# A third pair of FFN blocks as seven products, and both FFN projections in one sequence

## The chip, the cores and the metric

The kernel runs on one core of one Trainium2 chip. The metric is the device time of one execution in microseconds: 942.69 us is the median of three runs of the kernel before (941.98 to 943.01). Times inside an execution come from a profile of one run, counted from its first instruction (its span).

Names of the engines: PE is TensorE's matmul side and PEld its loading of the stationary operand, DVE is VectorE, ACT is ScalarE, POOL is GpSimd, SP is the engine whose queue issues the DMAs. L90 is line 90 of the kernel before.

## The reference

Two layers of a hybrid encoder over 256 tokens of width 1024, all in float32. A layer computes a combined projection, gated linear attention (GLA) and grouped-query attention, merges them, projects once more, and then does a feed-forward part (FFN) and an input embedding. What matters here is the FFN:

```python
def hybrid_layer(h, p_i, ...):
    ...
    gate, up = jnp.split(rms_norm(h, g_ffn_pre) @ w_ffn_in, 2, axis=-1)
    h = h + rms_norm((jax.nn.silu(gate) * up) @ w_ffn_out, g_ffn_post)

    e = p_i @ w_ple_proj
    h = h + rms_norm(jax.nn.sigmoid(h @ w_ple_gate) * e, g_ple_post)
    return h
```

The hidden width is 2816, so w_ffn_in is 1024 x 5632 (gate columns, then up columns) and w_ffn_out is 2816 x 1024.

## The kernel before, in words

**Precision.** Every float32 operand of a large matmul is split into a high and a low part (`split`, L104: a cast on ScalarE, L106, and a subtraction on VectorE, L102). A product is then three matmuls (`mm3`, L92): high by high, high by low, low by high. The tokens lie in two halves (hf 0 and 1) of 128, and an activation is the stationary operand: a matmul is 128x128 by 128x512.

**Weights.** `plan` (from L167) lists all weight units in the order of their use; a unit is 128 x 2048 numbers, 1 MB. `Stream` loads a unit by SP's queue into one of two raw buffers, splits it in two pieces of 1024 columns into a pair of buffers wh and wl (four of each), and hands it out with `take`; `done` frees the buffers and starts the split and the load of later units. Up to four units are held.

**FFN, first projection.** The hidden width is 11 blocks of 256 (`NBLK`). A plain block (`block`, L1219) takes 256 gate and 256 up columns as two units (one for each half of the contraction) and makes 48 matmuls of 512 columns; its results go through silu and a product (VectorE, L99), four 128x128 transposes on TensorE, and a split into `hid`, the transposed hidden state.

**Pairs.** Two blocks (b and b+1) can be done as one pair by Strassen's scheme in Winograd's form (`seven`, L559; `Stream.step`, L278): a 2x2 block product with seven products of 12 matmuls in place of eight. The seven weight operands are made from four loaded quarters by sums of 128 x 2048 on VectorE (L282 to L293), two of which lie in a wh and a wl buffer that is lent for them, one in a buffer of the pool `big`. The seven activation operands are quarters and four sums made once a layer (`sums`, L534). The products are combined by VectorE steps of 512 columns (L102, L566) and ScalarE copies (L583), and `gated` (L1251) turns each half into hidden state.

**The order.** Blocks 0 and 1 come first. Then `FFN_IN` (L35) is an order written out by hand: "u" is one unit of a plain block, the digits 1 to 7 are the products of a pair. `PLAIN` names the plain blocks (4, 5, 8, 9, 10), `PAIRS` the first blocks of the pairs (2 and 6). After it, rope_tables(l+1) and up_weights(l+1) make the next layer's small tables (layer 0 only), p is loaded and transposed (`turn_p_in`), and the second projection runs (`out_step`, L1294): 11 units, each with 12 matmuls for each half; the last four units are done by half, so that the post-norm of half 0 runs beside the matmuls of half 1.

**What else sets the order.** `tick` counts steps of TensorE's program; a `Task` does its next piece after the number of ticks that it yields (WAIT_PAIR is 9 ticks from a pair's gating to its transposes). Engine orders follow the program's order, except that work marked by `high_priority` goes earlier and work that is ready may be placed ahead of work that is not. Pools: `mid` has 10 buffers of 128 x 1024, `big` 9 of 128 x 2048, and PSUM 8 banks, shared by accumulators (`acc`) and transposes (`aux`).

Of the kernel before, what the change touches and what calls it, by code (L numbers as in the profile page):

```python
# [17 lines left out]
P = 128  # L18
T = 256
# [12 lines left out]
HIDDEN = 2816  # L32
NBLK = HIDDEN // 256

FFN_IN = "uu12u34u5u67uu12u34u5u67"  # L35
WAIT_PAIR = 9
PLAIN, PAIRS = (4, 5, 8, 9, 10), (2, 6)
UNIT = 2112
RQ = ((0, 288), (288, 672), (672, 1056))
C_GQ, C_GK, C_GV, C_GG, C_RA = 0, 512, 1024, 2048, 3072  # L40
# [4 lines left out]
def trunk_kernel(ctx: ExitStack, tc: tile.TileContext, a: dict, out: bass.AP):  # L45
# [107 lines left out]
    def unit_rows(w, n, c0=0, c1=D, parts=1):  # L153

        if parts == 2:
            return lambda t: [
                (t[:, k * (c1 - c0) : (k + 1) * (c1 - c0)], w[(2 * n + k) * P : (2 * n + k + 1) * P, c0:c1])
                for k in range(2)
            ]
        return lambda t: [  # L160
            (
                t[:, : 2 * (c1 - c0)].rearrange("p (k c) -> p k c", k=2),
                w[n * 256 : (n + 1) * 256, c0:c1].rearrange("(k p) c -> p k c", p=P),
            )
        ]

    plan = []  # L167
    for l in range(DEPTH):
        w = a["w_in"][l]
        plan += [unit_rows(w, n, C_RA, C_RA + 1056, 2 if l + n == 0 else 1) for n in range(4)]  # L170
        for c0 in (C_AK, C_GQ, C_GK, C_GV, C_GV + 512, C_GG, C_GG + 512, C_GA, C_GA + 512, C_GB, C_GB + 512):
            plan += [unit(w, kh, c0) for kh in range(2)]
        for j in range(2):
            for wo in (a["w_o_gla"][l], a["w_o_attn"][l]):
                plan += [unit(wo, kh, j * 512) for kh in range(2)]
        plan += [unit(a["w_out"][l], kh, j * 512) for kh in range(2) for j in range(2)]
        w = a["w_ffn_in"][l]
        blocks = [[unit_gate_up(w, kh, b) for kh in range(2)] for b in range(NBLK)]
        plan += blocks[0] + blocks[1]
        plains = [u for b in PLAIN for u in blocks[b]]  # L180
        pairs = [[unit(w, kh, c + b * 256) for kh in range(2) for c in (0, HIDDEN)] for b in PAIRS]
        for x in FFN_IN:
            if x == "1":
                pair = pairs.pop(0)
            plan.append(plains.pop(0) if x == "u" else (pair, int(x)))
        plan += [unit_rows(a["w_ffn_out"][l], n) for n in range(NBLK)]
        plan += [unit_rows(a["w_ple_proj"][l], 0)]
        plan += [unit(a["w_ple_gate"][l], kh, j * 512) for kh in range(2) for j in range(2)]

# [259 lines left out]
    def halves(t):  # L449
        return [t[:, j * 512 : (j + 1) * 512] for j in range(2)]  # L450
# [108 lines left out]
    def seven(sp, forms, gated):  # L559

        made, task = forms
        quad = lambda hf, j: lambda k: sp.tok(4 * j + k, hf)
        form = lambda i: lambda k: [p[:, k, :] for p in made[i]]

        def add(out, x, y):
            nc.vector.tensor_tensor(out=out, in0=x, in1=y, op=ALU.add)  # L566

        (p1, v), (p3, p7), (c12, c22) = (halves(mid()) for _ in range(3))
        c11 = acc()
        times(c11, quad(0, 0))  # L570
        nc.scalar.copy(p1, c11)
        yield
        task.need()
        o = acc()
        times(o, form(0))
        nc.scalar.copy(p3, o)
        yield
        p5 = acc()
        times(p5, form(1))
        yield  # L580
        o = acc()
        times(o, form(2))
        nc.scalar.copy(p7, o)  # L583
        yield
        o = acc()
        times(o, form(3))
        vsub(v, o, p1)
        add(v, p5, v)
        add(c12, v, p3)
        add(c22, v, p7)  # L590
        yield
        times(c11, quad(0, 1), False)
        gated(0, c11, c12)
        yield
        times(p5, quad(1, 1), False)
        vsub(v, p5, c22)
        gated(1, v, c22)
        yield
# [164 lines left out]
    for l in range(DEPTH):  # L763
# [399 lines left out]
        for j in range(2):  # L1163
            for br, src in enumerate((gT, aT)):
                for hf, o in enumerate(project(src)):
                    sl = [s[:, hf, j * 512 : (j + 1) * 512] for s in sgate]
                    vmul(sl[br], o, sl[br])
                    if br == 1:
# [5 lines left out]

                        mixT.makers[hf].append(Task(turn(), part[0], j))


        part[0] = f"{l}wout"
        gpost = gain(a["g_mix_post"][l], mid(), D)
# [70 lines left out]
        def pair(b):  # L1250
            def gated(hf, gate, up):  # L1251
                sg = t512()
                nc.scalar.activation(sg, gate, AF.Silu)
                vmul(sg, up, sg)
                turned(sg, 2 * b, 4, hf, WAIT_PAIR)

            return seven(u2, forms, gated)

        steps, pairs, seven_ = chain.from_iterable(block(b) for b in PLAIN), list(PAIRS), None
        for x in FFN_IN:  # L1260
            if x == "1":
                seven_ = pair(pairs.pop(0))
            next(steps if x == "u" else seven_)
        ws.lend = False

        if l + 1 < DEPTH:
            ropes = rope_tables(l + 1)
            wup_next = up_weights(l + 1)


        part[0] = f"{l}emb"
        pin = t512().rearrange("p (s c) -> p s c", c=256)
        nc.sync.dma_start(pin, a["p"][l, 0].rearrange("(s p) c -> p s c", p=P))
        pT = [t.rearrange("p (k t) -> p k t", t=T) for t in halves(mid(F32R))]

        def turn_p_in():
            yield 8
            ps = aux()
            for k in range(2):
                for hf in range(2):  # L1280
                    nc.tensor.transpose(
                        ps[:, k * T + hf * P : k * T + (hf + 1) * P], pin[:, hf, k * P : (k + 1) * P], ident
                    )
            split(pT[0], pT[1], ps.rearrange("p (k t) -> p k t", t=T))

        embedded = Task(turn_p_in(), part[0])


        part[0] = f"{l}ffnout"
        gpost = gain(a["g_ffn_post"][l], mid(), D)  # L1290
        gple = gain(a["g_ple_post"][l], mid(), D)
        o = [[acc(), acc()] for _ in range(2)]

        def out_step(n, hf, w):  # L1294
            wh, wl = (t[:, :2048].rearrange("p (k c) -> p k c", c=512) for t in w)
            for kk in range(2):
                k = 2 * n + kk
                hid.need(hf, k)
                for j in range(2):
                    mm3(  # L1300
                        o[hf][j], hid.tok(k, hf), (wh[:, 2 * kk + j, :], wl[:, 2 * kk + j, :]),
                        k == 0, k == 2 * NBLK - 1,
                    )
                tick()

        for n in range(NBLK - 4):
            w = ws.take()
            for hf in range(2):
                out_step(n, hf, w)
            ws.done()  # L1310
        us = [ws.take() for _ in range(4)]
        hT = Split()
        for hf in range(2):
            for n in range(4):
                out_step(NBLK - 4 + n, hf, us[n])
                if hf == 1:
                    ws.done()
            post_norm_add(o[hf], gpost, hf)

            turn_in(hT, h[:, hf, :], hf, WAIT_H)  # L1320
# [93 lines left out]
```

## Time and profile before

| What | us |
|---|---|
| median of three runs | 942.69 |
| the profiled execution, whole | 942.66 |
| its span, first to last instruction | 940.9 |
| chain of waits: TensorE's share | 85% |
| chain of waits: VectorE, DMA, ScalarE, POOL | 6%, 3%, 2%, 2% |
| one ScalarE cast of half a unit (128 x 1024) | 1.05 |
| one VectorE subtraction of half a unit | 1.22 |
| one VectorE sum of two quarters (128 x 2048) | 2.28 |
| landing of a 1 MB load of w_ffn_out | 4.8 to 6.4 |
| DMA, mean over the span | 180 GB/s |

In layer 0 the second pair's products run from 342.37 to 379.2 us, the second projection from 379.8 to 441.8 us. The chain of waits is the work that ended last, followed back step by step; the durations in the table are means of one instruction, and neighbours on an engine overlap by some 0.08 us.

### The profile page before, as it was taken

What the parts mean: (1) busy time and instruction counts of PE and PEld (TensorE: products, weight loads), DVE (VectorE), ACT (ScalarE), POOL (GpSimd) and SP (SyncE); (2) the same over time, 40 slices, a digit from 0 to 9 for tenths busy, and PEclk for the clock granted to TensorE, in tenths of its full rate; (3) what the DMA queues carried; (4) which work ended last, traced back from release to release, by engine and by line L of the source; (5) the groups of instructions that cost most, each with busy time, mean ns of one, the idle gap of its engine ahead of it and who ended that gap; (6) DMA issues with size and microseconds to landing.
All of it is one profiled execution on the core that took longest, in us unless ns stands there. A gap on an engine that the chain in (4) does not pass through costs nothing.

```text
span 940.9 us, 12357 instructions
## 1 busy us (share of the span) xinstructions
PE 927.7 (99%) x4721; PEld 788.9 (84%) x4721; DVE 695.6 (74%) x906; ACT 547.0 (58%) x916; POOL 90.2 (10%) x152
## 2 busy tenths in 40 slices
PE   8999999999999999999999999999999999999996
PEld 7998888888878888888889988888888788888886
DVE  5798977456679999755779799674666798996374
ACT  5569676434466666444656686754436656664263
POOL 3500211000000000301032001200002000000010
PEclk9999999999999999999999999999999999999999
DMA  7463444655385554764545525365552937276531
GB/s 256 140 240 120 162 173 170 216 181 191 102 279 178 185 182 155 264 245 157 181 138 179 194 76 179 121 237 184 206 190 92 311 125 261 75 265 227 179 135 45
DMA packets 92313, 169.26 MB, mean 180 GB/s; under 512 B 3479, under 2 KB 34711, under 8 KB 92254
## 3 DMA queue, kind: packets, MB, share of 16 engines
q1 hardware_dynamic: 92254, 168.47, 52.5%
q8 instruction: 37, 0.61, 0.3%
q14 instruction: 22, 0.18, 0.1%
HBM read 167.41 MB, written 1.05 MB: 179 GB/s over the span
## 4 chain that ended last, share of the span: by engine, by line
PE 85%; DVE 6%; DMA 3%; ACT 2%; POOL 2%; issue 2%; SPq 0%; POOLq 0%; DVEq 0%; ACTq 0%
PE acc_1ffnout L90 6%; PE acc_0ffnout L90 6%; PE acc_1ffnin L90 6%; PE acc_0ffnin L90 6%; PE acc_0gate L90 5%; PE acc_1gate L90 5%; PE acc_1merge L90 5%; PE acc_0merge L90 5%; PE acc_0ffnin L527 4%; PE acc_1ffnin L527 3%; PE acc_1gqk L90 2%; PE acc_0gqk L90 2%; PE acc_1ple L90 2%; PE acc_1gg L90 2%; PE acc_0gg L90 2%; PE acc_1v L90 2%
## 5 line engine op out<-in xcount | busy, mean ns | idle before, releaser
L90 PE MATMUL acc_1ffnin<-wh_1ffnin,big_1wout 128*128 128x512 f32 x160 | 51.8, 394 | 0.0
L90 PE MATMUL acc_0ffnin<-wh_0ffnin,big_0wout 128*128 128x512 f32 x160 | 51.8, 394 | 0.0
L106 ACT CAST wh_1ffnin<-raw_1ffnin 128x1024 fp32r<-128x1024 f32 x28 | 27.9, 1049 | 16.2 <-PE acc_1ffnin L90 8.8
L102 DVE TENSOR_TENSOR wl_1ffnin<-raw_1ffnin,wh_1ffnin 128x1024 fp32r<-128x1024 f32 x28 | 32.9, 1218 | 5.1 <-ACT wh_1ffnin L106 5.1
L106 ACT CAST wh_0ffnin<-raw_0ffnin 128x1024 fp32r<-128x1024 f32 x28 | 27.9, 1048 | 14.8 <-PE acc_0ffnin L90 9.3
L102 DVE TENSOR_TENSOR wl_0ffnin<-raw_0ffnin,wh_0ffnin 128x1024 fp32r<-128x1024 f32 x28 | 33.2, 1226 | 3.2 <-ACT wh_0ffnin L106 3.1
L90 PEld LDWEIGHTS acc_0ffnin<-wh_0ffnin,big_0wout 128*128 128x128 f32 x160 | 30.0, 188 | 6.1
L90 PEld LDWEIGHTS acc_1ffnin<-wh_1ffnin,big_1wout 128*128 128x128 f32 x160 | 30.0, 188 | 6.1
L90 PE MATMUL acc_0ffnout<-wh_0ffnout,big_0ffnin 128*128 128x512 f32 x112 | 34.9, 390 | 0.0
L90 PE MATMUL acc_1ffnout<-wh_1ffnout,big_1ffnin 128*128 128x512 f32 x112 | 34.9, 390 | 0.0
L102 DVE TENSOR_TENSOR wl_1ffnout<-raw_1ffnout,wh_1ffnout 128x1024 fp32r<-128x1024 f32 x18 | 21.3, 1221 | 16.5 <-ACT wh_1ffnout L106 16.5
L90 PE MATMUL acc_0ffnin<-wl_0ffnin,big_0wout 128*128 128x512 f32 x80 | 31.2, 390 | 0.0
L90 PE MATMUL acc_1ffnin<-wl_1ffnin,big_1wout 128*128 128x512 f32 x80 | 31.2, 390 | 0.0
L106 ACT CAST wh_1ffnout<-raw_1ffnout 128x1024 fp32r<-128x1024 f32 x18 | 18.1, 1051 | 20.8 <-PE acc_1ffnout L90 15.5
L102 DVE TENSOR_TENSOR wl_0ffnout<-raw_0ffnout,wh_0ffnout 128x1024 fp32r<-128x1024 f32 x18 | 21.3, 1220 | 11.4 <-ACT wh_0ffnout L106 11.3
L102 DVE TENSOR_TENSOR wl_1gate<-raw_1gate,wh_1gate 128x1024 fp32r<-128x1024 f32 x14 | 16.5, 1222 | 17.8 <-ACT wh_1gate L106 17.8
L102 DVE TENSOR_TENSOR wl_0gate<-raw_0gate,wh_0gate 128x1024 fp32r<-128x1024 f32 x14 | 16.5, 1221 | 17.8 <-ACT wh_0gate L106 17.8
L106 ACT CAST wh_0ffnout<-raw_0ffnout 128x1024 fp32r<-128x1024 f32 x18 | 18.1, 1053 | 15.0 <-PE acc_0ffnout L90 7.7
L90 PE MATMUL acc_0rq<-wh_start,big_start 128*128 128x384 f32 (+1 forms) x96 | 24.5, 339 | 1.0 <-ACT big_start L116 0.9
L90 PE MATMUL acc_1gate<-wh_1gate,big_0ple 128*128 128x512 f32 x80 | 24.8, 389 | 0.0
L90 PE MATMUL acc_0gate<-wh_0gate,big_start 128*128 128x512 f32 x80 | 24.8, 389 | 0.0
L90 PEld LDWEIGHTS acc_0ffnout<-wh_0ffnout,big_0ffnin 128*128 128x128 f32 x112 | 21.0, 188 | 4.4
(653 smaller groups left out, 3026.0 us busy)
## 6 DMA issues: line engine op xcount, KB each, us to landing
raw_0ffnin<-in_w_ffn_in_dram SPq DMA_DIRECT2D x16, 512.0 KB, 5.9
raw_1ffnin<-in_w_ffn_in_dram SPq DMA_DIRECT2D x16, 512.0 KB, 6.3
raw_0ffnin<-in_w_ffn_out_dram SPq DMA_DIRECT2D x6, 1024.0 KB, 5.3
raw_1ffnin<-in_w_ffn_out_dram SPq DMA_DIRECT2D x6, 1024.0 KB, 4.8
raw_0ffnout<-in_w_ffn_out_dram SPq DMA_DIRECT2D x5, 1024.0 KB, 6.4
raw_1ffnout<-in_w_ffn_out_dram SPq DMA_DIRECT2D x5, 1024.0 KB, 4.8
raw_0rq<-in_w_in_dram SPq DMA_DIRECT2D x4, 1024.0 KB, 5.0
raw_0v<-in_w_in_dram SPq DMA_DIRECT2D x4, 1024.0 KB, 4.9
```

The costliest lines, as they stand in the source:

```text
L90: return nc.tensor.matmul(o, lhsT, rhs, start=start, stop=stop)
L102: nc.vector.tensor_tensor(out=out, in0=in0, in1=in1, op=ALU.subtract)
L106: nc.scalar.copy(hi, src)
L527: nc.tensor.matmul(o, x, y, start=first and k + n == 0, stop=k == 3 and n == 2, skip_group_check=not first)
```

## The change

It makes blocks 8 and 9 a third pair, so that three plain blocks (4, 5, 10) and three pairs (2, 6, 8) remain. One string, `FFN`, holds the order of both projections: "o" is a unit of the second projection, "p" a point at which the post-norm's gain and p are loaded. Pairs two and three are laid between eight of the units of the second projection; the last three (7, 8, 9) are done by half. `OUT` is the order of the second projection's units, with unit 10 ahead of 6. The transposes of the last pair wait 3 ticks (half 0) and 4 ticks (half 1) instead of 9. A pair takes two `mid` buffers instead of three, since c12 and c22 are made in place of p3 and p7. rope_tables(l+1) is called ahead of the mixer's output projection, up_weights(l+1) after the sequence.

```diff
-FFN_IN = "uu12u34u5u67uu12u34u5u67"
-WAIT_PAIR = 9
-PLAIN, PAIRS = (4, 5, 8, 9, 10), (2, 6)
+FFN = "uu12u34u5u67" "uo12o34o5o67" "poo12o345o67"
+PLAIN, PAIRS = (4, 5, 10), (2, 6, 8)
+OUT = (0, 1, 2, 3, 4, 5, 10, 6, 7, 8, 9)
+WAIT_PAIR, WAIT_LAST = 9, (3, 4)
...
-        for x in FFN_IN:
+        outs = [unit_rows(a["w_ffn_out"][l], n) for n in OUT]
+        for x in FFN.replace("p", ""):
             if x == "1":
                 pair = pairs.pop(0)
-            plan.append(plains.pop(0) if x == "u" else (pair, int(x)))
-        plan += [unit_rows(a["w_ffn_out"][l], n) for n in range(NBLK)]
+            plan.append(plains.pop(0) if x == "u" else outs.pop(0) if x == "o" else (pair, int(x)))
+        plan += outs
...
-        (p1, v), (p3, p7), (c12, c22) = (halves(mid()) for _ in range(3))
+        (p1, v), (p3, p7) = (halves(mid()) for _ in range(2))
...
         add(v, p5, v)
+        c12, c22 = p3, p7
         add(c12, v, p3)
         add(c22, v, p7)
...
+        if l + 1 < DEPTH:
+            ropes = rope_tables(l + 1)
...
-                turned(sg, 2 * b, 4, hf, WAIT_PAIR)
+                turned(sg, 2 * b, 4, hf, WAIT_LAST[hf] if b == PAIRS[-1] else WAIT_PAIR)
...
+        for x in FFN:
+            if x == "p":
+                gpost = gain(a["g_ffn_post"][l], mid(), D)
+                pin = mid()[:, 0:512].rearrange("p (s c) -> p s c", c=256)
+                nc.sync.dma_start(pin, a["p"][l, 0].rearrange("(s p) c -> p s c", p=P))
+                pT = [t.rearrange("p (k t) -> p k t", t=T) for t in halves(mid(F32R))]
+                embedded = Task(turn_p_in(), f"{l}emb")
+                continue
+            if x == "o":
+                n, w = outs.pop(0), ws.take()
+                for hf in range(2):
+                    out_step(n, hf, w)
+                ws.done()
+                continue
+            if x == "1":
+                seven_ = pair(pairs.pop(0))
+            next(steps if x == "u" else seven_)
+        ws.lend = False
+
+        if l + 1 < DEPTH:
+            wup_next = up_weights(l + 1)
...
-        for n in range(NBLK - 4):
-            w = ws.take()
-            for hf in range(2):
-                out_step(n, hf, w)
-            ws.done()
-        us = [ws.take() for _ in range(4)]
+        us = [ws.take() for _ in outs]
         hT = Split()
         for hf in range(2):
-            for n in range(4):
-                out_step(NBLK - 4 + n, hf, us[n])
+            for n, w in zip(outs, us):
+                out_step(n, hf, w)
                 if hf == 1:
                     ws.done()
             post_norm_add(o[hf], gpost, hf)
```

The four accumulators of the second projection are taken at its first unit, so they are held through pairs two and three. turn_p_in waits 16 ticks instead of 8.

## The prediction

> **What bounds the kernel now.** I read the head of the page, then who waited for whom on TensorE, then the busy times by stretch of the first layer's feed-forward part, then VectorE's timeline where its second pair ends.
>
> ```profile
> span 940.9 us, 12357 instructions
> ...
> PE 927.7 (99%) x4721; PEld 788.9 (84%) x4721; DVE 695.6 (74%) x906; ACT 547.0 (58%) x916; POOL 90.2 (10%) x152
> ...
> PEld aux_0ple L397 <- DVE mid_0ple L447: 2.4, 2, 1.7
> ...
> PEld aux_1ffnin L1238 <- DVE t_1ffnin L99: 1.1, 3, 0.5
> ...
> PE acc_1ffnin L527 <- DVE mid_1ffnin L566: 0.2, 1, 0.2
> ```
>
> The waits' columns are total us, times, longest us. TensorE is busy all through, and in its whole table of waits no entry of a feed-forward part is over 1.1 us. So a matmul that falls away shortens the run by its spacing, as long as nothing new makes TensorE wait. The chain of waits gives the spacing:
>
> ```profile
> 305.82 5.44 PE acc_0ffnin L527 x24
> ...
> 348.94 5.44 PE acc_0ffnin L90 x24
> ```
>
> 24 matmuls take 5.44 us, 0.2267 us each (the groups' mean of 0.39 us is a latency: neighbours overlap). The page's share of 74% for VectorE is an average; by stretch it reads otherwise:
>
> ```profile
> core 0: us, PE busy (x) PEld busy (x) DVE busy (x) ACT busy (x) POOL busy (x), PEclk, DMA share, GB/s
> 282.60:331.20 48.60, 48.40 (x218) 39.39 (x217) 46.61 (x49) 31.24 (x41) 0.00 (x0) 1.00 0.57 189
> 331.20:379.80 48.60, 48.60 (x225) 40.20 (x224) 46.50 (x46) 30.52 (x39) 4.93 (x3) 1.00 0.49 166
> 379.80:438.00 58.20, 58.20 (x268) 48.32 (x268) 33.34 (x34) 27.27 (x33) 6.25 (x11) 1.00 0.60 208
> ```
>
> The first two rows are the two pairs (46.6 of 48.6 us, 96%), the third the second projection (57%). VectorE is thus close to being the bound beside the pairs, and has 25 us to spare behind them; the change moves work into that room.
>
> **The change, part by part.** *Matmuls.* Blocks 8 and 9 were plain, 2 x 48 matmuls; as a pair they are 7 products of 12, so 84. 12 fewer a layer, 24 in all: 24 x 0.2267 = **5.44 us less**. Transposes stay: two plain blocks put four 128x128 transposes each into one bank, a pair does so once for each half.
>
> *VectorE and ScalarE.* I take start-to-start times from the timeline:
>
> ```profile
> 372.94 0.68 DVE L566 TENSOR_TENSOR mid_0ffnin<-mid_0ffnin,mid_0ffnin 128x512 f32<-128x512 f32 x1
> 373.54 2.35 DVE L102 TENSOR_TENSOR wl_0ffnin<-raw_0ffnin,wh_0ffnin 128x1024 fp32r<-128x1024 f32 x2
> 375.81 0.68 DVE L566 TENSOR_TENSOR mid_0ffnin<-mid_0ffnin,mid_0ffnin 128x512 f32<-128x512 f32 x1
> 376.41 2.35 DVE L102 TENSOR_TENSOR wl_0ffnin<-raw_0ffnin,wh_0ffnin 128x1024 fp32r<-128x1024 f32 x2
> 378.68 0.42 DVE L99 TENSOR_TENSOR t_0ffnin<-acc_0ffnin,t_0ffnin 128x256 f32<-128x256 f32 x1
> 379.02 0.89 DVE L99 TENSOR_TENSOR t_0ffnin<-mid_0ffnin,t_0ffnin 128x512 f32<-128x512 f32 x1
> ```
>
> A split of a unit is 2.27 us (373.54 to 375.81), a 512-wide step 0.60, a 256-wide gating product 0.34, a 512-wide one 0.8; a sum of two weight blocks (lines 282 to 293) starts 2.2 us ahead of its successor (342.39 to 344.59). The new pair costs 7 splits in place of 4 (6.8), 4 weight sums (8.8), 5 steps that combine products (3.0) and 0.3 for the gating: 18.9 us of VectorE a layer. ScalarE gets 3 casts of a unit (2.0 each) and 3 copies (0.59): 7.8 us, beside a load of 63%; I cost that at nothing.
>
> Does VectorE hide it? By stretch of the new order, with 0.36 us for each group of four transposes on TensorE:
> - first twelve symbols: unchanged.
> - second (uo12o34o5o67): 12 splits 27.2, sums 8.8, the pair's own steps and the splits of its transposes 5.8, one plain block 1.3: 43.1 us against TensorE's 204 x 0.2267 + 1.1 = 47.3. Lighter than the same stretch before, which had two and a half plain blocks (45).
> - third (poo12o345o67): 11 splits 25.0, sums 8.8, 5.8, and 0.6 for p's input: 40.2 against 180 x 0.2267 + 1.1 = 41.9.
>
> So it fits on the whole, at 96%. Locally the tight place is "345o67" and the three units behind. I follow it from the second pair before (its first product at 342.37, the third's split at 348.38, the fourth's done at 355.13), counting from the first product: the fifth's split ends at 15.0, the sum behind it at 17.2, the o unit's split at 19.5, wanted at 20.2; the sixth's at 21.8 (25.6); the seventh's at 24.7 (28.3); the combining steps at 26.5 (28.3); the first last unit's at 28.7 (31.1). Then come the pair's own results, which unit 8 reads: product six ends at 28.3. Before, this product ended near 376.5 and its gating at 379.8, 3.3 us later; here the transposes stand behind product seven and half a unit of one half (2.72 + 1.36 = 4.1 us), so they are fed. Splits for units 8 and 9 end at 32.2 and 36.5, wanted at 34.1 and 36.9. Spare time is 0.3 to 0.7 us at the narrowest, and in layer 1 before, product seven once waited for a combining step (0.2 us in the row above, 0.6 from the last matmul). For these places together I take 0.5 us a layer, **1.0 us**; bounds: 0 (all fits) and 2.7 a layer (next part).
>
> *Order of moved work.* rope_tables(1) goes from behind the FFN to ahead of wout, layer 0 alone: four DMAs (two of 128 KB, two small) and 10 POOL operations, 9.5 us of POOL (375.82 to 385.2). The gain loads emitted at that very place went out far earlier:
>
> ```profile
> 133.86 0.50 SPq L323 DMA_DIRECT2D mid_0wout<-in_g_mix_post_dram  x1
> ...
> 147.19 0.50 SPq L323 DMA_DIRECT2D mid_0wout<-in_g_ffn_pre_dram  x1
> ```
>
> so I expect the tables near 134 to 150, where POOL makes the GLA norms that are needed 10 us and more later. Zero; if instead they sat ahead of the wout norms (POOL at 247.5 and 251.6), up to the first long operation, 3.5 us, once. The gain for the post-norm (512 KB) and p (256 KB) enter SP's queue ahead of the third stretch's loads: 0.77 MB on 8 MB in 42 us, 208 GB/s, which the third row above already moved; nothing, at most 0.77 MB / 208 GB/s = 3.7 us once a layer if a load is late. up_weights (six small DMAs, a ScalarE cast of 1.05, a VectorE step of 1.22) now stands 8 us (3 x 2.72) ahead of the first post-norm instead of 50 (379.3 to 429.5); its cast ran 16 us behind its place (395.0), so it may meet the second post-norm; half of one such step, **0.5 us**, bounds 0 and 2.3. PSUM: the four output accumulators leave four banks to a pair, which holds two, with one for a product and one for transposes; the split of a transposed tile took 2 us (379.2 to 381.1) against 2.72 us a product. Nothing. The last three units by half instead of four: the post-norm of half 0 is still followed by five ticks before its transposes. Nothing. In-place c12 and c22: same steps, fewer buffers.
>
> **Sum.** The profiled execution took 942.66 us (span 940.9, 1.8 outside), against a median of 942.69. 942.66 - 5.44 + 1.0 + 0.5 = **938.7 us**.
>
> **Rivals.** *The last pair's gating is late (slower).* By program order the gating product of product six stands behind the splits of all three last units. Held in that order it waits 3 x 2.27 + 0.8 = 7.6 us after product six, against 4.1 of cover: 3.5 us of TensorE waiting a layer. Such a wait has a second price, which the end of layer 0 shows: after gaps of 1.36 and 0.31 us
>
> ```profile
> 480.00:482.00 2.00, 0.75 (x5) 0.44 (x3) 0.70 (x2) 2.00 (x4) 0.87 (x2) 1.00 0.37 142
> ...
> 484.00:486.00 2.00, 2.00 (x8) 2.00 (x9) 2.00 (x3) 0.54 (x2) 0.00 (x0) 0.51 0.00 0
> 486.00:488.00 2.00, 2.00 (x11) 2.00 (x9) 0.25 (x1) 0.00 (x0) 0.00 (x0) 0.63 0.92 254
> ```
>
> the granted clock was 0.51 and 0.63 for two stretches, 1.7 us lost. So 942.66 - 5.44 + 2 x (3.5 + 1.7) = 947.6. It decides from 2.7 us a layer on. For it: 18.9 us more on an engine at 96%. Against it: in the timeline above the gating at 379.02 ran between two splits, not behind the third. Chance 0.17.
>
> The Trainium skill ("TensorE: Matmul & The Clock Gate", Part 1) says that the clock falls after an idle window of about 3.4 us; by that, this rival pays the clock only where its wait is long enough. The trace differs: less than 2 us of gaps were enough here.
>
> *VectorE takes the gain back (no change).* If the third stretch runs at the durations' plain sum, without the overlap of neighbours (1.22 twice a split, 2.29 a sum, 0.68 a step), it needs 26.8 + 9.2 + 6.4 + 0.7 = 43.1 us against 41.9, and the three last units and gatings another 1 us late: 2.2 us a layer. 942.66 - 5.44 + 4.4 + 0.5 = 942.1. Chance 0.16.
>
> *Nothing waits.* The second stretch's lighter VectorE also removes the small waits at L1238: 942.66 - 5.44 = 937.2 or, with 0.5 off, 936.7. Chance 0.17; the forecast keeps 0.50.
>
> That the change does not do what it says can be read off the count: TensorE should lose 24 of 4721.
>
> **How the numbers follow.** Range 936.6 to 944.0: it takes in the forecast, "nothing waits", "takes it back", and costs of up to 3.7 us once; what it leaves out is most of the slower rival. The likeliest case alone has 937.5 to 940.5. About 0.2% (1.9 us) is what a measurement of this kernel can tell from no change. Faster: the forecast and "nothing waits", 0.67, of which I keep 0.66. Slower: 0.18. Within: 0.16.
>
> **What would show it.** Right: TensorE 4697 instructions; VectorE near 733 us and ScalarE near 562; VectorE above 90% up to the last three units; no TensorE wait over 1 us in a feed-forward part; emb's first matmul about 2 us earlier behind wout in each layer. Wrong: TensorE waiting for L1253/L99's results (aux tiles of the last pair) or for splits of the last units, with a clock under 1.00 behind; POOL's rope operations beside wout's norms; raw loads that land after VectorE is free.

## The result, and the profile after

The changed kernel took 938.48 us (median of six runs, 937.18 to 939.98) against 942.82 us for the kernel before beside it (six runs, 940.30 to 943.33): a ratio of 0.9959, interval 0.9945 to 0.9973, 3.9 us less. The forecast was 938.7. The profiled execution took 937.18 us (span 935.5), the fastest of the six; line numbers are those of the changed kernel, four or so above the old ones (L90 is now L94, L99 is L103, L102 is L106). The head of its page:

```profile
span 935.5 us, 12336 instructions
...
PE 922.2 (99%) x4697; PEld 783.8 (84%) x4697; DVE 732.1 (78%) x932; ACT 561.4 (60%) x930; POOL 83.8 (9%) x152
```

TensorE has 24 matmuls fewer, VectorE 36.5 us more, as forecast (4697, near 733, near 562). The busy times by stretch of layer 0, in the columns named ahead of the prediction's stretches (length; PE, PEld, DVE, ACT, POOL; clock):

```profile
284.00:332.00 48.00, 47.82 (x215) 38.87 (x215) 46.05 (x47) 31.07 (x41) 0.00 (x0) 1.00 0.55 186
332.00:380.60 48.60, 48.60 (x222) 40.22 (x221) 44.46 (x42) 28.71 (x34) 0.00 (x0) 1.00 0.60 217
380.60:422.00 41.40, 41.40 (x190) 34.31 (x189) 39.39 (x36) 26.19 (x31) 0.95 (x1) 1.00 0.39 138
422.00:439.00 17.00, 17.00 (x85) 14.18 (x84) 15.36 (x18) 11.23 (x16) 0.87 (x2) 1.00 0.76 276
```

The third row is the last pair: VectorE is busy 39.4 of 41.4 us (95%), and TensorE all of them. The chain of waits there, asked for this stretch of layer 0, has nothing but TensorE in it:

```profile
402.95 8.19 PE acc_0ffnin L532 x36
411.14 5.44 PE acc_0ffnin L94 x24
416.58 5.44 PE acc_0ffnin L532 x24
422.02 1.37 PE acc_0ffnin L94 x6
423.39 0.44 PE aux_0ffnin L402 x4
423.83 4.12 PE acc_0ffnin L94 x18
```

24 matmuls still take 5.44 us, and the last pair's transposes (423.39) come in without a gap. What TensorE's weight loads waited for in layer 1's feed-forward part (total us, times, longest; the matmuls behind them lost less, 0.4 us for the first row):

```profile
PEld aux_1ffnin L1247 <- DVE t_1ffnin L103: 1.4, 2, 0.8
...
PEld aux_1ffnin L402 <- DVE t_1ffnin L103: 0.4, 1, 0.4
PEld acc_1ffnin L94 <- ACT big_1ffnin L110: 0.4, 1, 0.4
```

So VectorE's and ScalarE's results are late by fractions of a us. VectorE's timeline at the end of layer 0's sequence shows how little is to spare:

```profile
418.35 2.35 DVE L106 TENSOR_TENSOR wl_0ffnin<-raw_0ffnin,wh_0ffnin 128x1024 fp32r<-128x1024 f32 x2
420.62 0.68 DVE L103 TENSOR_TENSOR t_0ffnin<-mid_0ffnin,t_0ffnin 128x512 f32<-128x512 f32 x1
...
425.21 1.22 DVE L106 TENSOR_TENSOR mid_0ffnin<-mid_0ffnin,mid_0ffnin 17x1024 fp32r<-17x1024 f32 x1
```

The first row splits the first of the last three units, the second is the gating product of the last pair's product six, the third is up_weights' step. The gating runs between two splits (in layer 1 behind the second), not behind the third: the order that the slower rival needed did not come.

**Where the profiled execution gained.** Taking from each trace the first matmul of a stage's accumulators, the way from wout to emb (the feed-forward part and wout) took:

| kernel (profiled execution) | layer 0, us | layer 1, us |
|---|---|---|
| before | 207.2 | 207.6 |
| after | 204.5 | 205.2 |
| 12 matmuls fewer would make of before | 204.5 | 204.9 |

That is 2.7 and 2.4 us of the 5.5 by which the two profiled executions differ. Another 1.2 us lies where nothing was changed, from the second layer's first matmul to its gate projection (133.5 us before, 132.3 after), and 0.9 us was lost again ahead of the gate projection of layer 0 (first matmul at 142.7 before, 143.6 after, and anywhere from 141.8 to 144.6 in the experiments). The 2.7 and 2.4 us are the best case: the unaltered kernel profiled a second time (e9) gained 1.7 and 0.5 us there.

The 1.2 us go with the clock. The prediction showed it at 0.51 and 0.63 in two stretches behind the layer's end; after, the same place reads:

```profile
478.00:480.00 2.00, 1.00 (x6) 0.68 (x4) 0.45 (x1) 2.00 (x4) 0.87 (x2) 1.00 0.48 187
480.00:482.00 2.00, 1.42 (x9) 1.00 (x9) 2.00 (x3) 1.97 (x3) 0.00 (x0) 1.00 0.00 0
482.00:484.00 2.00, 1.81 (x11) 1.53 (x11) 2.00 (x4) 0.79 (x2) 0.00 (x0) 1.00 0.00 0
```

TensorE is idle for 1.00, 0.58 and 0.19 us in these rows, in all as much as before (1.25 and 0.52), and the clock stays at 1.00. Of the profiled executions of all kernels here, three took 133.5 to 133.6 us from the second layer's first matmul to its gate projection (before, e1, e7), and these are the three in which the granted clock falls there (to 0.50 or 0.51 in slices of 2 us); the rest took 132.2 to 132.4 us.

### The profile page after: what moved, and what is told of

It is laid out like the page before. It is cut to its first block, busy times and chain, and to the rows that moved or that the text cites. A ratio compares the mean times of both kernels' runs of the same rounds, so it can differ in the third digit from the quotient of the medians.

```text
span 935.5 us, 12336 instructions
## 1 busy us (share of the span) xinstructions
PE 922.2 (99%) x4697; PEld 783.8 (84%) x4697; DVE 732.1 (78%) x932; ACT 561.4 (60%) x930; POOL 83.8 (9%) x152
## 4 chain that ended last, share of the span: by engine, by line
PE 85%; DVE 6%; DMA 3%; ACT 2%; POOL 2%; issue 2%; SPq 0%; POOLq 0%; DVEq 0%; ACTq 0%
PE acc_0ffnin L94 11%; PE acc_1ffnin L94 8%; PE acc_0ffnin L532 6%; PE acc_1ffnin L532 5%; PE acc_1gate L94 5%; PE acc_0gate L94 5%; PE acc_0merge L94 5%; PE acc_1merge L94 5%; PE acc_1gqk L94 2%; PE acc_0rq L94 2%; PE acc_0gqk L94 2%; PE acc_1ple L94 2%; PE acc_1gg L94 2%; PE acc_0gg L94 2%; PE acc_0v L94 2%; PE acc_1v L94 2%
## 5 line engine op out<-in xcount | busy, mean ns | idle before, releaser
L94 PE MATMUL acc_1ffnin<-wh_1ffnin,big_1ffnin 128*128 128x512 f32 x176 | 56.9, 393 | 0.0
L94 PE MATMUL acc_0ffnin<-wh_0ffnin,big_0ffnin 128*128 128x512 f32 x176 | 56.9, 392 | 0.0
L106 DVE TENSOR_TENSOR wl_1ffnin<-raw_1ffnin,wh_1ffnin 128x1024 fp32r<-128x1024 f32 x38 | 44.9, 1220 | 3.8 <-ACT wh_1ffnin L110 3.6
L106 DVE TENSOR_TENSOR wl_0ffnin<-raw_0ffnin,wh_0ffnin 128x1024 fp32r<-128x1024 f32 x38 | 44.7, 1219 | 3.4 <-ACT wh_0ffnin L110 3.4
L94 PEld LDWEIGHTS acc_1ffnin<-wh_1ffnin,big_1ffnin 128*128 128x128 f32 x176 | 33.0, 188 | 7.0 <-ACT big_1ffnin L110 0.4
L94 PEld LDWEIGHTS acc_0ffnin<-wh_0ffnin,big_0ffnin 128*128 128x128 f32 x176 | 33.1, 188 | 6.7
L106 DVE TENSOR_TENSOR wl_1ffnin<-lent_1ffnin,wh_1ffnin 128x1024 fp32r<-128x1024 f32 x30 | 35.5, 1220 | 2.7 <-ACT wh_1ffnin L110 2.5
L106 DVE TENSOR_TENSOR wl_0ffnin<-lent_0ffnin,wh_0ffnin 128x1024 fp32r<-128x1024 f32 x30 | 35.5, 1219 | 1.9 <-ACT wh_0ffnin L110 1.7
L94 PE MATMUL acc_0ffnin<-wl_0ffnin,big_0ffnin 128*128 128x512 f32 x88 | 34.3, 389 | 0.0
L94 PE MATMUL acc_1ffnin<-wl_1ffnin,big_1ffnin 128*128 128x512 f32 x88 | 34.3, 389 | 0.0
L94 PE MATMUL acc_0ffnin<-wh_0ffnin,big_0wout 128*128 128x512 f32 x96 | 31.2, 395 | 0.0
L94 PE MATMUL acc_1ffnin<-wh_1ffnin,big_1wout 128*128 128x512 f32 x96 | 31.2, 395 | 0.0
L532 PE MATMUL acc_1ffnin<-wh_1ffnin,mid_1ffnin 128*128 128x512 f32 x96 | 31.0, 390 | 0.0
L532 PE MATMUL acc_0ffnin<-wh_0ffnin,mid_0ffnin 128*128 128x512 f32 x96 | 31.0, 390 | 0.0
L106 DVE TENSOR_TENSOR wl_1gate<-raw_1gate,wh_1gate 128x1024 fp32r<-128x1024 f32 x14 | 16.5, 1222 | 17.8 <-ACT wh_1gate L110 17.8
L106 DVE TENSOR_TENSOR wl_0gate<-raw_0gate,wh_0gate 128x1024 fp32r<-128x1024 f32 x14 | 16.5, 1221 | 17.8 <-ACT wh_0gate L110 17.8
L94 PE MATMUL acc_0rq<-wh_start,big_start 128*128 128x384 f32 (+1 forms) x96 | 25.3, 348 | 0.9 <-ACT big_start L120 0.9
L94 PE MATMUL acc_0gate<-wh_0gate,big_start 128*128 128x512 f32 x80 | 24.8, 389 | 0.0
```

The lines of the kernel that those rows point to most:

```text
L94: return nc.tensor.matmul(o, lhsT, rhs, start=start, stop=stop)
L106: nc.vector.tensor_tensor(out=out, in0=in0, in1=in1, op=ALU.subtract)
L532: nc.tensor.matmul(o, x, y, start=first and k + n == 0, stop=k == 3 and n == 2, skip_group_check=not first)
```

## The experiments

Times are medians; the ratio to the kernel before, from runs on the same chip, is what is compared. "Slower than after" means against 0.9959, times 943 us; by the intervals of the two ratios such a difference is uncertain by some 1.5 to 2 us. Each diff is against the changed kernel. Each profile is of one execution, and a stage of one kernel can differ by 1 to 2 us between two executions, as e9 shows.

**e1: the sequence without the third pair.** Blocks 8 and 9 are plain again, 4721 matmuls; both pairs' transposes wait 9 ticks, as before.

```diff
-FFN = "uu12u34u5u67" "uo12o34o5o67" "poo12o345o67"
-PLAIN, PAIRS = (4, 5, 10), (2, 6, 8)
+FFN = "uu12u34u5u67" "uo12o34o5o67" "poouuouuo"
+PLAIN, PAIRS = (4, 5, 10, 8, 9), (2, 6)
...
-                turned(sg, 2 * b, 4, hf, WAIT_LAST[hf] if b == PAIRS[-1] else WAIT_PAIR)
+                turned(sg, 2 * b, 4, hf, WAIT_PAIR)
```

> The changed kernel with blocks 8 and 9 plain again: one sequence, the same eight units of the second projection, the moved rope tables, but two pairs. Theory (the gain is the 24 matmuls alone, 24 x 0.2267 = 5.4 us, and the one sequence is worth nothing by itself): the time of the kernel before, 942 to 943.5. Rival (part of the gain comes from the sequence and from the moved tables, since VectorE is lighter in the second stretch): 939.5 to 941.

943.34 us, ratio 1.0003 (0.9993 to 1.0012). The mixed order by itself brings nothing and costs nothing, within 1 us: the gain is the 24 matmuls. From 1.0003 to 0.9959 is 4.1 us of their 5.44; some 1.3 us is given back somewhere (by the intervals 0 to 3).

**e2: the pairs without units between their products.** All products of pairs two and three stand in a row.

```diff
-FFN = "uu12u34u5u67" "uo12o34o5o67" "poo12o345o67"
+FFN = "uu12u34u5u67" "uo1234567" "poo1234567ooooo"
...
-                turned(sg, 2 * b, 4, hf, WAIT_LAST[hf] if b == PAIRS[-1] else WAIT_PAIR)
+                turned(sg, 2 * b, 4, hf, WAIT_PAIR)
```

> Three pairs, as many matmuls as in the changed kernel, but pairs two and three stand with their seven products in a row, and the units of the second projection behind them. Theory (the units between the products are what lets VectorE keep up): a bare pair needs 7 x 2.27 + 8.8 + 5.8 = 30.5 us of VectorE beside 19.0 + 0.7 of TensorE; less some 5 us that the splits run ahead, 5 to 6 us of waiting for each of four bunched pairs, and up to 1.7 us of lower clock behind each: 958 to 970. Rival (only VectorE's total counts, which is unchanged): 937 to 940.

952.85 us, 1.0105 (1.0090 to 1.0120): 13.8 us slower than after. The waits of TensorE's weight loads and a window over the last pair of layer 0:

```profile
PEld acc_0ffnin L532 <- DVE wl_0ffnin L106: 3.4, 3, 1.6
...
PEld acc_0ffnin L94 <- DVE wl_0ffnin L106: 2.7, 2, 1.3
```

```profile
385.00:425.00 40.00, 37.33 (x167) 29.76 (x166) 37.44 (x37) 24.73 (x29) 0.00 (x0) 1.00 0.44 154
```

Each operand of a product costs VectorE a split and most of them a sum as well; with no unit of another kind between, a weight load waits up to 1.6 us for one. The direction was right, the size too large by 5 us or more: in gaps that add up to 2.7 of 40 us the clock stayed at 1.00 (0.999 over the run), so no second price came on top. The longer wait of the last pair's transposes is in this run too; its share was not measured.

**e3: the last pair's transposes wait 9 ticks, as for other pairs.**

```diff
-WAIT_PAIR, WAIT_LAST = 9, (3, 4)
+WAIT_PAIR, WAIT_LAST = 9, (9, 9)
```

> The changed kernel with the last pair's transposes 9 ticks behind its gating, as for the other pairs. They are then forced at the point of use, unit 8, for both halves, and TensorE waits for transpose, cast and subtraction, which took 2 us before (379.2 to 381.1). Theory: one such wait of 1.3 to 2 us for each half and layer, so 5 to 8 us more than the changed kernel, 943.5 to 947, the whole gain. Rival (TensorE finds other work, as the transposes go ahead when they are ready): 938 to 939.5.

942.40 us, 0.9991 (0.9982 to 1.0000): 3.0 us slower than after, between the theory's 5 to 8 and the rival's 1.5. In its profile (944.24 us, the slowest of its eleven runs) TensorE waits 0.6 us for the last pair's hidden state, in layer 1 alone, and then for the post-norm's result, 1.4 us in layer 1 and 0.7 in layer 0; the first profile of after has none of the three. So the theory had the place, but most of the price came one step later, at the post-norm. The short wait is a part of the change that pays, at less than the size expected.

**e4: rope_tables back behind the sequence.**

```diff
-        if l + 1 < DEPTH:
-            ropes = rope_tables(l + 1)
...
         if l + 1 < DEPTH:
             wup_next = up_weights(l + 1)
+            ropes = rope_tables(l + 1)
```

> The changed kernel with the rope tables made behind the FFN sequence, beside the up weights. Theory (moving them cost nothing and hides nothing that matters, unless POOL's 8 to 10 us meet the post-norm's two short POOL operations, 8 us behind that place): 938 to 941.5, with the delay at the post-norm of half 0 in layer 0, visible as a late POOL row. Rival (they go early on their own, as the gain loads did, so that the place makes no difference): within 0.5 us of the changed kernel.

941.35 us, 0.9980 (0.9972 to 0.9989): 2.0 us slower than after. In its profile layer 0 took 207.9 us from wout to emb, 3.4 more than in the first profile of after (layer 1 205.6, 0.4 more). The forecast time held, the reason given for it did not: the post-norm was not held up by POOL. POOL took the tables at 405 to 416 us, in the middle of the last pair. Its timeline and VectorE's in this kernel:

```profile
409.78 6.16 POOL L656 TENSOR_TENSOR rope_0ffnin<-mid_0ffnin 128x64 f32<-128x64 f32 x4
```

```profile
409.25 2.72 DVE L298 TENSOR_TENSOR lent_0ffnin<-lent_0ffnin,raw_0ffnin 128x2048 f32<-128x2048 f32 x1
411.89 5.14 DVE L106 TENSOR_TENSOR wl_0ffnin<-raw_0ffnin,wh_0ffnin 128x1024 fp32r<-128x1024 f32 x4
```

and the same instructions in the changed kernel:

```profile
159.61 1.18 POOL L656 TENSOR_TENSOR rope_0merge<-mid_0merge 128x64 f32<-128x64 f32 x4
```

```profile
406.68 2.29 DVE L298 TENSOR_TENSOR lent_0ffnin<-lent_0ffnin,raw_0ffnin 128x2048 f32<-128x2048 f32 x1
408.89 4.62 DVE L106 TENSOR_TENSOR wl_0ffnin<-raw_0ffnin,wh_0ffnin 128x1024 fp32r<-128x1024 f32 x4
```

Beside one another both get longer: VectorE's sum and four split halves by 0.43 and 0.52 us, POOL's four products from 1.18 to 6.16. TensorE's waits in layer 0 say how much of the loss this is (in brackets the idle time before, and what ended it):

```profile
330.61 0.47 PE L532 MATMUL acc_0ffnin<-wh_0ffnin,big_0wout 128*128 128x512 f32 x1 [0.82 <-DVE mid_0ffnin L571]
...
348.61 0.55 PE L1244 MATMUL aux_0ffnin<-ident,t_0ffnin 128*128 128x128 f32 x3 [0.77 <-DVE t_0ffnin L103]
...
429.83 0.96 PE L94 MATMUL acc_0ffnin<-wh_0ffnin,big_0ffnin 128*128 128x512 f32 x3 [1.00 <-DVE big_0ffnin L106]
```

The third, 1.00 us behind the last pair, fits the 0.95 us that VectorE lost beside POOL. The first two stand 50 us and more ahead of the tables, whose loads are issued from 398.9 us on, so it is not the tables that cause them; the first is a place where another execution waits too (e9). So about half of the 2.0 us is accounted for by POOL and VectorE holding each other up; where the rest comes from is not shown, and with the intervals there need not be any.

**e5 and e6: one suspected cost doubled.** VectorE makes the low part of the last pair's sixth operand twice (e5) or three times (e6): 2.27 and 4.54 us more of VectorE a layer, nothing else.

```diff
-                self.made(q)
+                self.pairs_done = getattr(self, "pairs_done", 0) + 1
+                for hi, lo, raw in self.put(q):
+                    split(hi, lo, raw)
+                    for _ in range(1 if self.pairs_done % 3 == 0 else 0):
+                        vsub(lo, raw, hi.bitcast(F32))
```

e6 has `range(2 ...)` in the fifth line.

> The changed kernel with the low part of the last pair's sixth weight operand made twice (the same result): 2.27 us more of VectorE once a layer, in the tight place. Theory (the last units' splits have some 0.1 to 1.3 us to spare there): TensorE waits 1 to 2 us in layer 0 and 0.3 to 1.5 us in layer 1: 1.3 to 3.5 us more than the changed kernel. Rival (the splits run ahead by whole units, several us to spare): within 0.5 us of the changed kernel.

> As the kernel with the low part made twice, but three times: 4.54 us more of VectorE once a layer. Theory (beyond the small room every us of VectorE is a us of waiting): 2 x 2.27 = 4.5 us above the kernel with one repetition, and up to 1.7 us of lower clock for each wait over 2 us: 5 to 11 us above the changed kernel. Rival (several us to spare): 0 to 2 us above it.

e5: 943.71 us, 0.9989 (0.9980 to 0.9997), 2.8 us slower than after. e6: 948.90 us, 1.0037 (1.0024 to 1.0049), 4.5 us slower than e5. Both lie in the ranges of their theories. The second step costs just what it adds to VectorE (2 x 2.27), the first 2.8 of 4.5: the spare time at the last pair is (4.5 - 2.8) / 2, some 0.9 us a layer (with intervals of about 1 us on each ratio, a rough figure). Past that VectorE sets the end. The two layers need not have the same room: in e5's profile layer 1 took 207.1 us from wout to emb, as in e9 without the extra step, and layer 0 206.9 against 205.5. In layer 1 the extra step fills time in which VectorE waits for a load in e9 (1.81 us); in e5 it has no idle time there.

**e7: a fourth pair.** Blocks 4 and 5 become a pair as well, 24 matmuls fewer again.

```diff
-FFN = "uu12u34u5u67" "uo12o34o5o67" "poo12o345o67"
-PLAIN, PAIRS = (4, 5, 10), (2, 6, 8)
-OUT = (0, 1, 2, 3, 4, 5, 10, 6, 7, 8, 9)
+FFN = "uu1234567" "oo12o34567" "poo12o34567" "o12o34567"
+PLAIN, PAIRS = (10,), (2, 4, 6, 8)
+OUT = (0, 1, 10, 2, 3, 4, 5, 6, 7, 8, 9)
```

> The same step once more: blocks 4 and 5 as a pair too, four pairs, block 10 plain, the units of the second projection spread over the four (order 0, 1, 10, 2, 3, 4, 5, 6, then 7, 8, 9 by half). TensorE saves another 24 x 0.2267 = 5.4 us, VectorE gets another 18.9 us a layer. Theory (the room is used up): VectorE needs some 36.3, 37.3, 37.9 and 35 us in the four stretches against 30.6, 36.1, 36.1 and 30.6 of TensorE, 13 us too much a layer, less some 4 that the splits run ahead: 945 to 960. Rival (TensorE's count decides as before): 932 to 934.

957.44 us, 1.0129 (1.0114 to 1.0145): 16 us slower than after, with 5.4 us less of matmuls, and inside the theory's range. A window over layer 0's sequence has VectorE busy for 172 of 180 us, and TensorE, which set the time before, idle for 8.7 us of them:

```profile
269.60:449.60 180.00, 171.33 (x764) 137.33 (x765) 172.08 (x167) 111.99 (x142) 1.82 (x3) 1.00 0.54 192
```

**e8: the fourth pair, with two of each pair's four weight sums on POOL.** On top of e7:

```diff
-                nc.vector.tensor_tensor(out=x.raw[:, c], in0=x.raw[:, c], in1=z.raw[:, c], op=ALU.add)
+                nc.gpsimd.tensor_tensor(out=x.raw[:, c], in0=x.raw[:, c], in1=z.raw[:, c], op=ALU.add)
...
-                nc.vector.tensor_tensor(out=z.raw[:, c], in0=z.raw[:, c], in1=y.raw[:, c], op=ALU.add)
+                nc.gpsimd.tensor_tensor(out=z.raw[:, c], in0=z.raw[:, c], in1=y.raw[:, c], op=ALU.add)
```

> The four pairs, with the first two of the four weight sums of each pair on POOL. A rope product of 128x256 took 0.74 us there, so a sum of 128x2048 is some 5.9 us, an estimate from that row. VectorE loses 4.4 us a pair, 35 us in all. Theory (VectorE is the bound of the four pairs): 936 to 948, below the four pairs on VectorE alone by 5 to 15 us. Rival (POOL and VectorE hold each other up when both read two operands from SBUF, or the sums come late for the third and fourth operands): no better than the four pairs on VectorE, with longer VectorE subtractions in the rows.

994.91 us, 1.0528 (1.0514 to 1.0543): the theory fell, its rival was right. POOL's and VectorE's timelines at the first two of these sums:

```profile
291.37 4.61 POOL L287 TENSOR_TENSOR lent_0ffnin<-lent_0ffnin,lent_0ffnin 128x2048 f32<-128x2048 f32 x1 [23.28 <-DVE wl_0ffnin L106]
296.05 4.90 POOL L290 TENSOR_TENSOR lent_0ffnin<-lent_0ffnin,big_0ffnin 128x2048 f32<-128x2048 f32 x1
```

```profile
291.49 5.04 DVE L106 TENSOR_TENSOR mid_0ffnin<-t_0ffnin,mid_0ffnin 128x512 fp32r<-128x512 f32 x1
296.45 5.59 DVE L106 TENSOR_TENSOR wl_0ffnin<-big_0ffnin,wh_0ffnin 128x1024 fp32r<-128x1024 f32 x1
```

A subtraction of 512 columns takes 5.04 us where it takes 0.68 otherwise, one of 1024 columns 5.59 instead of 1.22: they end 0.6 and 1.1 us behind the POOL sums beside them. These two sums stopped VectorE for nearly all of their time. The Trainium skill ("SBUF — State Buffer", "SBUF: two separate sides") says that the two share a port pair as an exclusive lock, held for a whole instruction, and that a VectorE operation with two SBUF inputs contends with POOL operations that read SBUF. These rows agree with it. Such sums need not be all of the some 38 us that e8 loses against e7: TensorE's weight loads wait up to 4.7 us at a time, and the granted clock falls in the feed-forward parts (0.64 and 0.68 from 300 to 310 us, 0.979 over the run). How the loss divides was not measured.

**e9: the changed kernel once more**, unaltered.

> The changed kernel again, beside two variants of its end. Theory (5.44 us of matmuls less, some 1 to 1.5 us of small waits): a ratio of 0.9952 to 0.9963 to the kernel before, 938.5 to 939.5 where the kernel before takes 943. Rival (no waits): 0.9942.

939.93 us, 0.9960 (0.9946 to 0.9974). The ratio repeats; its profiled execution is 2.8 us longer than the first one, and so shows what the remaining waits are. Wout to emb took 205.5 us in layer 0 and 207.1 in layer 1. The table of waits of TensorE's weight loads has for layer 1:

```profile
PEld aux_1ffnin L402 <- DVE t_1ffnin L103: 2.0, 1, 2.0
PEld acc_1ffnin L532 <- ACT t_1ffnin L1262: 1.1, 1, 1.1
```

The timelines of SP, ScalarE, VectorE and TensorE at the first of these, a row or two each:

```profile
871.46 10.40 SPq L257 DMA_DIRECT2D raw_1ffnin<-in_w_ffn_out_dram  x3
```

```profile
878.02 2.00 ACT L110 CAST wh_1ffnin<-raw_1ffnin 128x1024 fp32r<-128x1024 f32 x2 [4.60 <-DMA raw_1ffnin<-in_w_ffn_out_dram]
```

```profile
879.10 2.36 DVE L106 TENSOR_TENSOR wl_1ffnin<-raw_1ffnin,wh_1ffnin 128x1024 fp32r<-128x1024 f32 x2 [1.81 <-ACT wh_1ffnin L110]
...
884.86 0.68 DVE L103 TENSOR_TENSOR t_1ffnin<-mid_1ffnin,t_1ffnin 128x512 f32<-128x512 f32 x1
```

```profile
885.59 0.66 PE L402 MATMUL aux_1ffnin<-ident,t_1ffnin 128*128 128x128 f32 x4 [1.56 <-DVE t_1ffnin L103]
```

Read from the top: the load of the first of the last three units is issued at 871.46 and has landed when its cast starts, 6.6 us later. VectorE, the engine with 0.9 us to spare, stands idle for 1.81 us; the splits behind run that much later, and the gating product, laid behind two of them, ends when TensorE has waited for it. In the first execution the same load was issued at 870.28 and its cast started 5.0 us later:

```profile
875.29 2.00 ACT L110 CAST wh_1ffnin<-raw_1ffnin 128x1024 fp32r<-128x1024 f32 x2 [3.04 <-DMA raw_1ffnin<-in_w_ffn_out_dram]
```

The profiles of e10 and e11 below have the same wait at the same place: VectorE idle for 2.11 and 1.81 us, then TensorE for 1.86 and 1.67 us (1.56 here). In layer 1 the landing of one 1 MB load decides on it; the matmuls of layer 0 do not wait there in any of the four profiles. The load is issued no earlier since its raw buffer is not free: of the two, the pair's fourth quarter (q) holds one.

The second row of the table is a smaller wait of another place, the end of the first pair, whose order the change leaves alone:

```profile
789.30 0.47 PE L532 MATMUL acc_1ffnin<-wh_1ffnin,big_1wout 128*128 128x512 f32 x1 [0.67 <-ACT t_1ffnin L1262]
```

It is product seven that waits. The profile names the silu of product six, which ends last (789.26 us); it stood as close behind product six in the first execution, where nothing waited, so what is late is the combining step behind product five (L571), which ends at 789.15 and is named in the other profiles. The wait was 0.2 us in layer 1 before, and lies between 0 and 0.9 us a layer in the profiles of the changed order. In e9 a load, of w_ffn_in, is behind it as well: ScalarE's cast waits 1.35 us for the load, VectorE 0.85 us for the cast.

**e10: up_weights behind the last three units.** It takes VectorE's 1.22 us out of the end of layer 0's sequence.

```diff
-        if l + 1 < DEPTH:
-            wup_next = up_weights(l + 1)
-
         us = [ws.take() for _ in outs]
...
+        if l + 1 < DEPTH:
+            wup_next = up_weights(l + 1)
```

> The changed kernel with up_weights (layer 0: a ScalarE cast of 1.05 us and a VectorE step of 1.22 us) made behind the last three units, out of the tight place. Theory (its step at 425.2 stands ahead of the last pair's gating and the last unit's split, where nothing is to spare): 0.3 to 1.2 us less than the changed kernel. Rival (it sits in a gap): the same.

941.07 us, 0.9973 (0.9962 to 0.9983): not faster than after, a miss. Layer 0 took 205.5 us from wout to emb, as in e9, so its end did not wait for that step; in its new place the step may cost 0.5 us (30.6 us from emb to the next layer's first matmul, against 30.1 in the first profile of after). In layer 1, which does not make these tables, the wait for the gating was there again (2.3 us of a weight load, once).

**e11: the same, and p and the gain loaded in the second stretch** instead of ahead of the third.

```diff
-FFN = "uu12u34u5u67" "uo12o34o5o67" "poo12o345o67"
+FFN = "uu12u34u5u67" "uo12po34o5o67" "oo12o345o67"
```

> As the one with up_weights later, and p's load, transposes and split in the second stretch, which has more room on VectorE (44.2 of 48.3 us against 39.4 of 41.4). Theory: another 0 to 0.6 us a layer less, since VectorE loses 0.6 us in the tight stretch. Rival: the same, as p's split ran in a gap of VectorE (403.68 to 405.4).

939.86 us, 0.9962 (0.9946 to 0.9977): the same as after. That these loads were in anybody's way is not seen.

**e12: the pair's fourth quarter into the pool big.** Both raw buffers then serve the units.

```diff
-                        y, q = Load(b22, big), Load(b21)
+                        y, q = Load(b22, big), Load(b21, big)
...
-                self.load()
+                self.start()
```

> The kernel after, with each pair's fourth quarter loaded into a buffer of the pool big instead of one of the two raw buffers, so that both raw buffers serve the plain units and the second projection's units while a pair runs. Theory (the remaining 1.5 us over the matmuls' term come from the first last unit's load, which is issued late because the fourth quarter holds a raw buffer, so its split and with it the last pair's gating are late): that load is issued several us earlier, ScalarE's cast of it no longer waits for a DMA, and the run takes 0.5 to 2 us less than the kernel after: ratio 0.9940 to 0.9957. Rival (VectorE's own order of splits and gating decides, the load only fills its gap): the load is earlier, the same waits for the gating stay, and the ratio is that of the kernel after, 0.9957 to 0.9968. Second rival (a load that is issued earlier competes with others, or the pool big has no buffer to spare): 0.9970 or more.

937.84 us against 943.66, 0.9938 (0.9924 to 0.9952): 2.0 us less than after, a little below the theory's range, and the best kernel of this study. SP's queue, ScalarE, VectorE and TensorE at the place of the rows above:

```profile
839.99 15.68 SPq L257 DMA_DIRECT2D raw_1ffnin<-in_w_ffn_out_dram  x2
```

```profile
874.71 3.91 ACT L110 CAST wh_1ffnin<-raw_1ffnin 128x1024 fp32r<-128x1024 f32 x4 [2.58 <-DVE wl_1ffnin L106]
```

```profile
881.66 0.68 DVE L103 TENSOR_TENSOR t_1ffnin<-mid_1ffnin,t_1ffnin 128x512 f32<-128x512 f32 x1
```

```profile
882.40 0.65 PE L402 MATMUL aux_1ffnin<-ident,t_1ffnin 128*128 128x128 f32 x4
```

The second of the two issues in the first row is the load in question: it goes out at 855.3, some 15 us earlier. ScalarE's cast no longer waits for a DMA, the gating product is done before the transposes are due, and they follow without an idle time. Wout to emb is 204.3 us in layer 1, 3.3 less than before the change. In layer 0 it is 205.3 us. Apart from those for wout's splits at the start of the feed-forward part (0.7 us in layer 0, 0.2 in layer 1), the table has no wait of a matmul in either. As to the size, the intervals of e12 and of after overlap (0.9945 to 0.9952), so the runs leave it open between nearly nothing and 4 us; that the wait is gone is read from the one profile.

## Why the prediction was right, point by point

**Matmuls, 5.44 us less: right.** e1 shows that nothing else in the change brings time by itself, and in the first profile the feed-forward part of layer 0 is shorter by just 12 spacings. With e12, where little waits, the whole kernel gains 5.8 us (943.66 - 937.84; by the interval 4.5 to 7.2).

**VectorE's room: right.** The second stretch was put at 43.1 us of VectorE in 47.3, the third at 40.2 in 41.9; the profile has 44.5 in 48.6 and 39.4 in 41.4. That it would be the next bound is shown by e5 and e6: 0.9 us a layer to spare, and us for us behind it. The 0.3 to 0.7 us worked out from the old timeline was the right order. e2 and e7 show the same bound where the units between the products, or the number of plain blocks, no longer cover it.

**The narrow places, 1.0 us, and up_weights, 0.5 us: the sum right, its parts only in half.** e1 against after leaves some 1.3 us given back, near the 1.5 of the forecast. But up_weights costs nothing that e10 could show. The wait of product seven for a combining step, which the prediction named, is there, at the first pair (0.2 and 0.7 us in e9's two layers); at the last pair the larger wait is not among its combining steps but comes from the first unit behind it, whose load lands late (1.6 to 1.9 us of layer 1 in three profiles of four). That one term that fell away and one that was missing nearly cancel is luck. Of the signs that the prediction named for being right, "no TensorE wait over 1 us" held in the first profile and not in e9's.

**The loads, costed at nothing: the step that was mis-sized.** The prediction looked at bytes (208 GB/s, already moved before the change) and gave a late load at most 3.7 us. The queue's rate was no limit; the raw buffer was. The load could have gone out 15 us earlier; issued late, it was there for its cast 5 to 6.6 us after its issue, and VectorE had to wait for it. In e12, where it goes out early, the wait is gone. It was listed there as a sign to look for; it deserved a term of its own, some 1.5 us, once and not in each layer.

**rope_tables, moved at no cost: right, and half the story.** SP's queue issued their loads where the prediction put them:

```profile
134.75 0.50 SPq L646 DMA_DIRECT2D mid_0merge<-in_rope_cos_dram  x1
...
148.07 0.51 SPq L328 DMA_DIRECT2D mid_0merge<-in_g_q_norm_dram  x1
```

From the first matmul of the gate projection to that of wout it is 91.9 us in both profiles. What was not seen is that the move is a condition of a part of the gain: left behind the sequence the tables cost 2.0 us (e4), about half of it because POOL lengthens VectorE's steps where VectorE is the tight engine.

**The rivals.** "Nothing waits" came out in layer 0 of the first profiled execution and nearly in e12. "VectorE takes the gain back" is what e5 makes of the kernel (0.9989). "The last pair's gating is late" named the right place: there the largest remaining wait sits, 1.6 us in one layer of e9, not 3.5 in both, and it follows from a late load, not from program order alone. Its second price, the clock, did not come: no feed-forward stretch of after, e2 or e7 shown here is below 1.00. It did come in e8, where the waits are longer.

**What stays open.** Which executions drop the clock at the layer's end, and so whether the 1.2 us there in the first comparison are more than chance, is not known. The size of what e12 gains is open too, and what makes the first pair's wait differ between executions.

## What to carry to other kernels

When an edit trades one engine's work for another's, measure the new engine's spare time at the tightest place (make one of its steps twice, then three times), since the average says little there: here 95% busy meant 0.9 us. At such a place look first at what feeds that engine, above all at which buffer lets the next load be issued, not only at the bytes moved. And keep work that makes its steps longer, here POOL's beside VectorE's, out of that stretch.

## What the runs showed of the hardware that was not expected

- A VectorE operation with two SBUF inputs beside a POOL sum of 128x2048 lasted as long as that sum: 5.04 us for 0.68, 5.59 for 1.22 (e8); four POOL products of 128x64 beside VectorE's splits took 6.16 us for 1.18 (e4).
- The landing of 1 MB loads differs between executions of one kernel: the medians for the second projection's weights, from the table of DMA issues in the page of the profile, were 5.3 us in layer 1 of the first execution and 6.1 us in that of e9.
- The same kind of gaps (1.8 us in all) at the layer's end dropped the granted clock in three profiles and left it at 1.00 in the others. The Trainium skill ("TensorE: Matmul & The Clock Gate", Part 1) says that the activity window is free-running, so that the clock's transition at a kernel's start depends on where in the window the first matmul lands. That the same holds for a gap is a guess; it would fit a drop that comes and goes. The threshold of about 3.4 us of idleness that the Trainium skill gives there does not fit, since less than 2 us were enough before the change.
